# Fourteen elementwise instructions of a two-branch decoder layer moved from VectorE to GpSimd

## Chip, cores and metric

The kernel runs on one core of a Trainium2 chip. The metric is the device time of one execution in microseconds (us). Engines are called as the profile calls them: PE (TensorE, matrix products; PEld is its weight load), DVE (VectorE), ACT (ScalarE), POOL (GpSimd), SP (SyncE, which issues the DMAs). They run side by side, each through its own list of instructions in order, and wait for each other by semaphores.

## What is computed

One layer with two token mixers over the same input, 256 positions by 2048 features, in fp32:

```python
h = rms_norm(x, norm_g)
proj = h @ w_in                                   # (256, 2048) @ (2048, 11264)
q, k, v, z_a, u_b, v_b, z_b, g_a, g_b = split(proj)
att = moba_attention(rms(q), rms(k), v)           # 8 heads, causal, one block here
y_a = (att * silu(z_a)) @ w_proj_a
sgu = gelu(u_b) * (W_s @ rms(gelu(v_b)) + b_s)    # the spatial gating unit
y_b = (sgu * silu(z_b)) @ w_proj_b
merged = sigmoid(g_a) * y_a + sigmoid(g_b) * y_b
return x + merged @ w_out
```

The change touches three elementwise lines of it: the product `gelu(u_b) * mixed`, the product of that with `silu(z_b)`, and the sum of the two gated branches.

## The kernel before

**Products in three parts.** Every weight and every activation is split into a rounded half and the rest (`wh` and `wl`, `xh` and `xl`), and a product is three matrix instructions that accumulate in PSUM. ACT makes the rounded half by a cast (L125, L152, L154), DVE the rest by a subtraction (L126, L155, L157).

**The stream of quads.** The weights come as a stream of pieces of 128 x 2048, 1 MB each, numbered 0, 1, 2, ... by `schedule()`; the number stands in the buffers' names (`wl63`, `tl62`). A quad is four blocks of 128 x 512. Some quads are multiplied directly, 24 instructions (`direct`). The others go through one level of Strassen-Winograd (`seven`, L321), 21 instructions, for which DVE first adds the blocks (`t`: L143, L145, L146) and then makes three remainders: `wlp` (L155) and the two pieces of `tl` (L157), each of 128 x 1024. A direct quad costs DVE one instruction (L126, 128 x 2048), a Strassen quad six.

**Stages.** The columns come in the order q, k, v, za, vb, ub, zb, eight quads each. Then four chunks of 512 output columns follow: eight quads of the two gates (`g`, five of them Strassen) and four pieces of `proj`, the products with w_proj_a and w_proj_b. Last come two rounds of `out`. `early` (L346 to L353) and `final_one` (L361) put together the results of the Strassen quads on DVE.

**The three places of the change.** `spatial` (L491 to L494) multiplies four tiles of 128 x 512 during stage zb. `gate_b` (L496 to L499) multiplies four tiles during the first gate chunk; its result is transposed on PE and split (`turn_z`, L502) in the first `proj`. `merge` (L527 to L536) multiplies both branches with their gates and adds them, two sums in each of four chunks. Their result is transposed by `turn_m` behind the last `proj`.

**What sets the order.** Work is recorded quad by quad in the loop at the end of `hybrid_layer_kernel`. After quad 8 a scheduler decides on each engine's order from its own model of the times, so an edit on one engine can also move instructions on another. The buffers bound how far the engines run ahead: four for `raw` and `t` together, three for `wh` and `th`, three for `wl` and `tl`, two for `whp` and `wlp`.

The four remainders and blocks that the text below names are made here:

```python
nc.scalar.copy(wh[i], r[:, B:])
for sl in (a, b):
    nc.scalar.copy(th[i][:, sl], t[:, sl])
nc.vector.tensor_tensor(wl[i], r[:, B:], f(wh[i]), op=ALU.subtract)
for sl in (a, b):
    nc.vector.tensor_tensor(tl[i][:, sl], t[:, sl], f(th[i][:, sl]), op=ALU.subtract)
```

Of the kernel before, what the change touches and what calls it, by code (L numbers as in the profile page):

```python
# [17 lines left out]
ALU = mybir.AluOpType  # L18
# [49 lines left out]
def hybrid_layer_kernel(  # L68
# [9 lines left out]
    nc = tc.nc  # L78
# [80 lines left out]
    X = {}  # L159
# [331 lines left out]
    def spatial():  # L491
        for m in range(2):
            for c in range(2):
                nc.vector.tensor_tensor(X["ub"][m][c], X["ub"][m][c], X["vb"][m][c], op=ALU.mult)  # L494

    def gate_b():  # L496
        for m in range(2):
            for c in range(2):
                nc.vector.tensor_tensor(X["zb"][m][c], X["zb"][m][c], X["ub"][m][c], op=ALU.mult)  # L499

    def halves(dst_h, dst_l, ps):
        nc.scalar.copy(dst_h, ps)  # L502
# [25 lines left out]
    def merge(c, Y):  # L528

        g = X["g", c]  # L530
        for m in range(2):
            nc.vector.tensor_tensor(g[m][0], Y[m], g[m][0], op=ALU.mult)
        for m in range(2):
            nc.vector.tensor_tensor(g[m][1], Y[2 + m], g[m][1], op=ALU.mult)
            nc.vector.tensor_tensor(g[m][0], g[m][0], g[m][1], op=ALU.add)
        X["m", c] = [g[0][0], g[1][0]]  # L536

    def mm_rows(acc, hl, i, kts, k0, first, last, by_row=False):
# [78 lines left out]
    at(i0 + 0, mix, None)  # L617
    at(i0 + 1, func, "ub", AF.Gelu_apprx_tanh)
    at(i0 + 2, spatial)
    i0 = first["g", 0]  # L620
    at(i0 + 1, func, "zb", AF.Silu)
    at(i0 + 2, gate_b)
    at(first["proj", 0] + 0, turn_z, "zb", "late")
    at(first["proj", 3] + 1, turn_m, 0, "L01")
# [33 lines left out]
    for i, (kind, name, c, kp, n) in enumerate(G):  # L658
# [41 lines left out]
        elif kind == "proj":  # L700
            if n % 2 == 0:
                Y = (Y if n else []) + [bank(E[n + m], f"y{n}_{c}{m}") for m in range(2)]
            z = ("za", "zb")[n // 2]

            def hl(k, m):
                return (X[z + "h"][:, k, m * P:(m + 1) * P], X[z + "l"][:, k, m * P:(m + 1) * P])

            mm_rows(Y[n // 2 * 2:], hl, i, None, 4 * (n % 2), n % 2 == 0, n % 2 == 1)
            if n == 3:
                merge(c, Y)  # L710
# [68 lines left out]
```

## Time and profile before

| what | value |
|---|---|
| runs of the kernel, median | 672.03 us (three: 668.34, 672.03, 673.25) |
| the profiled execution's own time | 668.8 us |
| its span, first to last instruction | 667.0 us |
| mean granted clock of PE, share of full speed | 0.997 |
| PE busy | 655.3 us (98%) |
| DVE busy | 614.2 us (92%) |
| ACT busy | 427.0 us (64%) |
| POOL busy | 32.1 us (5%), 28 instructions |

The span of one execution is what the trace shows; the execution's own time is 1.8 us longer, for what lies around the first and last instruction. A busy PE counts the modelled, overlapping ends of its matmuls, so its waits are better read from the starts of neighbouring instructions.

### The profile page before, as it was taken

What the parts mean: (1) busy time and instruction counts of PE and PEld (TensorE: products, weight loads), DVE (VectorE), ACT (ScalarE), POOL (GpSimd) and SP (SyncE); (2) the same over time, 40 slices, a digit from 0 to 9 for tenths busy, and PEclk for the clock granted to TensorE, in tenths of its full rate; (3) what the DMA queues carried; (4) which work ended last, traced back from release to release, by engine and by line L of the source; (5) the groups of instructions that cost most, each with busy time, mean ns of one, the idle gap of its engine ahead of it and who ended that gap; (6) DMA issues with size and microseconds to landing.
All of it is one profiled execution on the core that took longest, in us unless ns stands there. A gap on an engine that the chain in (4) does not pass through costs nothing.

```text
span 667.0 us, 7852 instructions
## 1 busy us (share of the span) xinstructions
PE 655.3 (98%) x2982; PEld 539.3 (81%) x2982; DVE 614.2 (92%) x605; ACT 427.0 (64%) x562; POOL 32.1 (5%) x28
## 2 busy tenths in 40 slices
PE   8899999999999999999999999999999999999997
PEld 4687788878888888888887888888888888888886
DVE  4499999899999699999999999989979989998996
ACT  7778968856995579674656845554564556746360
POOL 1000501300001004000000000000000000000000
PEclk9899999999999999999999999999999999999999
DMA  8962574455455615744545644845573474747641
GB/s 310 421 225 95 215 255 177 169 220 179 157 200 191 252 65 188 259 178 171 207 146 220 269 167 149 324 151 188 193 294 116 187 273 167 252 143 290 203 185 63
DMA packets 21925, 135.32 MB, mean 203 GB/s; under 512 B 2432, under 2 KB 3072, under 8 KB 6656
## 3 DMA queue, kind: packets, MB, share of 16 engines
q1 hardware_dynamic: 20736, 132.73, 53.8%
q10 hardware_dynamic: 1152, 2.10, 1.0%
q8 instruction: 23, 0.38, 0.2%
q14 instruction: 14, 0.11, 0.0%
HBM read 132.72 MB, written 2.10 MB: 202 GB/s over the span
## 4 chain that ended last, share of the span: by engine, by line
PE 48%; DVE 29%; ACT 8%; issue 8%; DMA 5%; POOL 1%; SPq 0%; DVEq 0%; ACTq 0%
PE acc_g L303 13%; PE y L303 11%; PE acc_out L303 9%; PE seven_g L303 6%; DVE tl L157 6%; DVE wl L126 5%; DMA raw<-in_w 5%; DVE t L143 3%; PE seven_out L303 3%; DVE wlp L155 3%; PE acc_vb L303 3%; ACT wh L125 3%; DVE t L145 2%; DVE t L146 2%; PE seven_vb L303 2%
## 5 line engine op out<-in xcount | busy, mean ns | idle before, releaser
L154 ACT CAST th<-t 128x1024 fp32r<-128x1024 f32 x104 | 109.2, 1053 | 114.5 <-DVE t L143 52.2
L126 DVE TENSOR_TENSOR wl<-raw,wh 128x2048 fp32r<-128x2048 f32 (+2 forms) x75 | 156.0, 2087 | 27.5 <-ACT wh L125 27.2
L125 ACT CAST wh<-raw 128x2048 fp32r<-128x2048 f32 (+2 forms) x75 | 130.8, 1751 | 54.8 <-PE acc_g L303 23.4
L157 DVE TENSOR_TENSOR tl<-t,th 128x1024 fp32r<-128x1024 f32 x104 | 126.1, 1217 | 3.9 <-ACT th L154 3.9
L155 DVE TENSOR_TENSOR wlp<-raw,whp 128x1536 fp32r<-128x1536 f32 x52 | 91.0, 1750 | 4.4 <-ACT whp L152 4.4
L152 ACT CAST whp<-raw 128x1536 fp32r<-128x1536 f32 x52 | 76.8, 1481 | 28.0 <-DMA raw<-in_w 13.0
L143 DVE TENSOR_TENSOR t<-raw 128x1024 f32<-128x1024 f32 x52 | 63.2, 1216 | 0.2
L303 PE MATMUL acc_g<-wh,xh 128*128 128x512 f32 x96 | 37.4, 389 | 0.0
L303 PE MATMUL acc_g<-wh,xl 128*128 128x512 f32 x96 | 37.3, 389 | 0.0
L303 PE MATMUL acc_g<-wl,xh 128*128 128x512 f32 x96 | 37.0, 389 | 0.0
L146 DVE TENSOR_TENSOR t<-t,raw 128x512 f32<-128x512 f32 x52 | 35.8, 689 | 0.3
L145 DVE TENSOR_TENSOR t<-t,raw 128x512 f32<-128x512 f32 x52 | 35.8, 689 | 0.2
L239 POOL TENSOR_TENSOR rs<-ms,mhalf 128x4 f32<-128x4 f32 x12 | 23.7, 1991 | 124.9 <-DVE ms L238 124.9
L303 PE MATMUL acc_q<-wl,xuh 128*128 128x512 f32 x64 | 26.1, 408 | 2.0 <-DVE wl L126 2.0
L303 PE MATMUL acc_q<-wh,xuh 128*128 128x512 f32 x64 | 25.6, 400 | 1.5 <-ACT wh L125 1.5
L303 PE MATMUL acc_q<-wh,xul 128*128 128x512 f32 x64 | 25.9, 404 | 0.8 <-ACT wh L125 0.8
L303 PE MATMUL y<-wh,zbl 128*128 128x512 f32 x64 | 25.1, 392 | 0.0
L303 PE MATMUL y<-wh,zal 128*128 128x512 f32 x64 | 25.0, 390 | 0.0
L303 PE MATMUL y<-wh,zah 128*128 128x512 f32 x64 | 25.0, 390 | 0.0
L303 PE MATMUL y<-wl,zah 128*128 128x512 f32 x64 | 24.9, 389 | 0.0
L303 PE MATMUL y<-wh,zbh 128*128 128x512 f32 x64 | 24.9, 389 | 0.0
L303 PE MATMUL y<-wl,zbh 128*128 128x512 f32 x64 | 24.9, 389 | 0.0
(502 smaller groups left out, 1599.9 us busy)
## 6 DMA issues: line engine op xcount, KB each, us to landing
raw<-in_w SPq DMA_DIRECT2D x117, 1024.0 KB, 4.8
raw<-in_w SPq DMA_DIRECT2D x5, 512.0 KB, 7.7
xnat<-in_x SPq DMA_DIRECT2D x2, 1024.0 KB, 12.7
xres<-in_x ACTq DMA_DIRECT2D x8, 256.0 KB, 4.9
xt<-in_xT SPq DMA_DIRECT2D x3, 512.0 KB, 9.6
out<-out_c SPq DMA_DIRECT2D x5, 256.0 KB, 2.5
raw<-in_w SPq DMA_DIRECT2D x2, 256.0 KB, 4.6
ws<-in_wsT SPq DMA_DIRECT2D x2, 256.0 KB, 2.9
```

What stands on the lines that cost most here:

```text
L125: nc.scalar.copy(h, r)
L126: nc.vector.tensor_tensor(l, r, f(h), op=ALU.subtract)
L143: nc.vector.tensor_tensor(two, r[:, B:3 * B].rearrange("p (a n) -> p a n", a=2), r[:, None, 0:B].to_broadcast([P, 2, B]), op=ALU.add)
L145: nc.vector.tensor_tensor(t[:, 2 * B:3 * B], t[:, 0:B], r[:, 2 * B:3 * B], op=ALU.add)
L146: nc.vector.tensor_tensor(t[:, 3 * B:], t[:, 2 * B:3 * B], r[:, 3 * B:], op=ALU.add)
L152: nc.scalar.copy(wh[i], r[:, B:])
L154: nc.scalar.copy(th[i][:, sl], t[:, sl])
L155: nc.vector.tensor_tensor(wl[i], r[:, B:], f(wh[i]), op=ALU.subtract)
L157: nc.vector.tensor_tensor(tl[i][:, sl], t[:, sl], f(th[i][:, sl]), op=ALU.subtract)
L239: nc.gpsimd.tensor_tensor(dst, ms[:, :n], mhalf[:, :n], op=ALU.pow)
L303: nc.tensor.matmul(acc, a, b, start=(start and n == 0), stop=(stop and n == 2))
```

## The change

Three `nc.vector` calls become `nc.gpsimd` calls: four instructions in `spatial`, four in `gate_b`, and the two sums of `merge` in chunks 0, 1 and 2. In chunk 3 the two sums stay on DVE. Tiles, arithmetic and DMAs are as before.

```diff
     def spatial():
         for m in range(2):
             for c in range(2):
-                nc.vector.tensor_tensor(X["ub"][m][c], X["ub"][m][c], X["vb"][m][c], op=ALU.mult)
+                nc.gpsimd.tensor_tensor(X["ub"][m][c], X["ub"][m][c], X["vb"][m][c], op=ALU.mult)
 
     def gate_b():
         for m in range(2):
             for c in range(2):
-                nc.vector.tensor_tensor(X["zb"][m][c], X["zb"][m][c], X["ub"][m][c], op=ALU.mult)
+                nc.gpsimd.tensor_tensor(X["zb"][m][c], X["zb"][m][c], X["ub"][m][c], op=ALU.mult)
...
         for m in range(2):
             nc.vector.tensor_tensor(g[m][1], Y[2 + m], g[m][1], op=ALU.mult)
-            nc.vector.tensor_tensor(g[m][0], g[m][0], g[m][1], op=ALU.add)
+            (nc.vector if c == 3 else nc.gpsimd).tensor_tensor(g[m][0], g[m][0], g[m][1], op=ALU.add)
```

On DVE, in the middle of the first gate chunk, the four products of `gate_b` stand before among the instructions that prepare quads 60 and 61 (t, wlp, tl and their numbers):

```order
L146 TENSOR_TENSOR t60_2780<-t60_2780,raw60_2743 128x512
L499 TENSOR_TENSOR zb0_c11_2646<-zb0_c11_2646,ub0_c11_2313 128x512
L499 TENSOR_TENSOR zb0_c12_2649<-zb0_c12_2649,ub0_c12_2316 128x512
L157 TENSOR_TENSOR tl60_2787<-t60_2780,th60_2786 128x1024
L499 TENSOR_TENSOR zb0_h_2647<-zb0_h_2647,ub0_h_2314 128x512
L499 TENSOR_TENSOR zb0_c22_2648<-zb0_c22_2648,ub0_c22_2315 128x512
L143 TENSOR_TENSOR t61_2821<-raw61_2778 128x1024
L155 TENSOR_TENSOR wlp61_2826<-raw61_2778,whp61_2825 128x1536
```

Now the same place of DVE's order reads:

```order
L146 TENSOR_TENSOR t60_2780<-t60_2780,raw60_2743 128x512
L155 TENSOR_TENSOR wlp61_2826<-raw61_2778,whp61_2825 128x1536
L157 TENSOR_TENSOR tl60_2787<-t60_2780,th60_2786 128x1024
L143 TENSOR_TENSOR t61_2821<-raw61_2778 128x1024
L145 TENSOR_TENSOR t61_2821<-t61_2821,raw61_2778 128x512
```

The four products are gone from here, and the preparation of quad 61 has closed up. From the start to the second piece of `tl62`, DVE's list holds the same instructions as before less the eight of `spatial` and `gate_b`; that second piece still stands behind `wl63`.

On PE, near the end of the same chunk, quad 62 is the last Strassen quad and quad 63 the direct quad behind it. Before, this is what leads up to the first use of the second piece of `tl62`, the last row here:

```order
L303 MATMUL seven_g0_1_2750<-th62_2867,xl0_424 128x512
L303 MATMUL seven_g0_1_2750<-th62_2867,xh0_423 128x512
L303 MATMUL acc_g0_2_2717<-th62_2867,xl1_349 128x512
L303 MATMUL acc_g0_2_2717<-th62_2867,xh1_348 128x512
L303 MATMUL acc_g0_3_2718<-wh63_2898,xl1_349 128x512
L303 MATMUL acc_g0_3_2718<-wh63_2898,xh1_348 128x512
L303 MATMUL acc_g0_0_2715<-wl63_2899,xh1_348 128x512
L303 MATMUL acc_g0_0_2715<-wh63_2898,xl1_349 128x512
L303 MATMUL acc_g0_0_2715<-wh63_2898,xh1_348 128x512
L303 MATMUL acc_g0_0_2715<-wl63_2899,xh1_348 128x512
L303 MATMUL acc_g0_1_2716<-wl63_2899,xh1_348 128x512
L303 MATMUL seven_g0_1_2750<-tl62_2868,xh0_423 128x512
```

Now PE's order there is the plain one; the second piece of `tl62` is first used in the third row from the end:

```order
L303 MATMUL seven_g0_3_2752<-th62_2867,xl0_424 128x512
L303 MATMUL seven_g0_3_2752<-th62_2867,xh0_423 128x512
L303 MATMUL seven_g0_3_2752<-tl62_2868,xh0_423 128x512
L303 MATMUL seven_g0_2_2751<-th62_2867,xl0_424 128x512
L303 MATMUL seven_g0_2_2751<-th62_2867,xh0_423 128x512
L303 MATMUL seven_g0_2_2751<-tl62_2868,xh0_423 128x512
L303 MATMUL seven_g0_1_2750<-th62_2867,xl0_424 128x512
L303 MATMUL seven_g0_1_2750<-th62_2867,xh0_423 128x512
L303 MATMUL seven_g0_1_2750<-tl62_2868,xh0_423 128x512
L303 MATMUL acc_g0_2_2717<-th62_2867,xl1_349 128x512
```

Thirteen products that stood ahead of the second piece of `tl62` now stand behind it: eleven of quad 63 and two of `acc_g0_2` with `th62`. Counted to the end of the program, 1,290 of the 2,724 products of L303 stand at or behind its first use before, and 1,303 now. SP's order is the same in both. On POOL the fourteen instructions follow each other, behind everything that POOL did before. ACT's order changes by single places.

## Rows read from the trace of the kernel before

**Rows 1.** The page's first part: busy time of each engine, share, instructions.

```profile
PE 655.3 (98%) x2982; PEld 539.3 (81%) x2982; DVE 614.2 (92%) x605; ACT 427.0 (64%) x562; POOL 32.1 (5%) x28
```

**Rows 2.** Busy time of each engine in stretches: from:to, length, engines, clock, DMA.

```profile
core 0: us, PE busy (x) PEld busy (x) DVE busy (x) ACT busy (x) POOL busy (x), PEclk, DMA share, GB/s
...
320.00:340.00 20.00, 20.00 (x90) 16.57 (x89) 19.90 (x22) 13.12 (x13) 0.00 (x0) 1.00 0.45 165
340.00:360.00 20.00, 19.41 (x87) 15.74 (x86) 19.93 (x22) 8.66 (x8) 0.00 (x0) 1.00 0.44 159
360.00:370.00 10.00, 9.68 (x43) 7.70 (x42) 9.66 (x7) 8.15 (x6) 0.00 (x0) 1.00 0.92 359
...
392.00:432.00 40.00, 40.00 (x179) 33.10 (x178) 38.70 (x37) 21.28 (x18) 0.00 (x0) 1.00 0.63 233
...
454.00:494.00 40.00, 40.00 (x178) 33.14 (x177) 37.03 (x36) 21.32 (x18) 0.00 (x0) 1.00 0.63 237
```

**Rows 3.** Timeline of PE, end of the first gate chunk: start, duration, instruction, idle before.

```profile
358.45 0.39 PE L303 MATMUL seven_g<-wlp,xh 128*128 128x512 f32 x1
359.43 0.50 PE L303 MATMUL seven_g<-th,xl 128*128 128x512 f32 x1 [0.59 <-ACT th L154]
...
360.94 0.73 PE L303 MATMUL seven_g<-tl,xh 128*128 128x512 f32 x2 [0.32 <-DVE tl L157]
361.50 0.39 PE L303 MATMUL acc_g<-wh,xl 128*128 128x512 f32 x1
...
364.93 0.39 PE L303 MATMUL seven_g<-tl,xh 128*128 128x512 f32 x1
```

**Rows 4.** Timeline of DVE, stages zb and first gate chunk.

```profile
293.24 0.68 DVE L145 TENSOR_TENSOR t<-t,raw 128x512 f32<-128x512 f32 x1
293.85 1.75 DVE L155 TENSOR_TENSOR wlp<-raw,whp 128x1536 fp32r<-128x1536 f32 x1
...
331.37 0.68 DVE L361 TENSOR_TENSOR zb_c<-acc_zb,zb_c 128x512 f32<-128x512 f32 x1
...
339.31 1.21 DVE L157 TENSOR_TENSOR tl<-t,th 128x1024 fp32r<-128x1024 f32 x1
...
345.59 1.28 DVE L499 TENSOR_TENSOR zb_c<-zb_c,ub_c 128x512 f32<-128x512 f32 x2
346.79 1.22 DVE L157 TENSOR_TENSOR tl<-t,th 128x1024 fp32r<-128x1024 f32 x1
...
363.43 1.22 DVE L157 TENSOR_TENSOR tl<-t,th 128x1024 fp32r<-128x1024 f32 x1
```

**Rows 5.** Groups of POOL: line, form, count | busy us, mean ns | idle before.

```profile
L217 POOL TENSOR_SCALAR_AFFINE_SELECT tri_f<-tri_f 128x512 f32<-128x512 f32 x1 | 0.6, 636 | 0.0
```

**Rows 6.** Instructions on tile ws: count, duration ns min/median/max, first and last start.

```profile
L228 POOL TENSOR_SCALAR_AFFINE_SELECT ws<-ws x2: 1082/1774/2466, 199.5 to 201.9; 128x512 f32<-128x512 f32 x2
```

**Rows 7.** Timeline of DVE beside those two POOL instructions.

```profile
199.07 1.21 DVE L157 TENSOR_TENSOR tl<-t,th 128x1024 fp32r<-128x1024 f32 x1
200.21 1.21 DVE L143 TENSOR_TENSOR t<-raw 128x1024 f32<-128x1024 f32 x1
201.46 1.01 DVE L145 TENSOR_TENSOR t<-t,raw 128x512 f32<-128x512 f32 x1
202.50 1.00 DVE L146 TENSOR_TENSOR t<-t,raw 128x512 f32<-128x512 f32 x1
203.43 1.21 DVE L157 TENSOR_TENSOR tl<-t,th 128x1024 fp32r<-128x1024 f32 x1
```

**Rows 8.** Timeline of ACT: the inputs of the moved products, and the reader of gate_b.

```profile
291.82 2.23 ACT L489 ACTIVATE vb_c<-ps_m,xv 128x128 f32<-128x128 f32 x8
...
330.29 1.23 ACT L403 ACTIVATE zb_c<-zb_c 128x512 f32<-128x512 f32 x2 [2.79 <-DVE zb_c L361]
...
332.08 0.63 ACT L403 ACTIVATE zb_c<-zb_c 128x512 f32<-128x512 f32 x1
...
375.60 1.06 ACT L502 CAST zbh<-ps_zb 128x512 fp32r<-128x512 f32 x2
```

**Rows 9.** Timeline of PE, first use of the second piece of tl58.

```profile
341.00 0.39 PE L303 MATMUL seven_g<-tl,Fhx 128*128 128x512 f32 x1
```

## Prediction

> **What bounds the kernel now.** I read the page's busy shares first. PE is busy 98% of the span and DVE 92% [rows 1]. With two engines that full, the question is where PE waits for DVE, so I went on to the table of stretches. From 320 to 370 us DVE is full (19.90 of 20, 19.93 of 20, 9.66 of 10), and PE loses 0.59 us in 340 to 360 and 0.32 us in 360 to 370. From 392 us on PE is busy in all of each stretch, while DVE has 1.30 us to spare in 392 to 432 and 2.97 us in 454 to 494 [rows 2]. So there is one place behind the middle of the program at which DVE is late: the end of the first gate chunk. Behind it PE sets the time.
>
> PE's timeline shows that place. The products of 128 x 512 follow each other every 0.23 us (fifteen starts from 361.50 up to the one at 364.93 us). Between 358.45 and 361.50 us there are seven starts (two in the row of 360.94), which take 7 x 0.23 = 1.61 us when nothing waits, but 3.05 us pass. PE loses 1.44 us, first to a cast of ACT and then to `tl` of DVE [rows 3]. What DVE does from 280 us to this place carries through to here, for it has no idle time to swallow a delay.
>
> The later piece of the same tile matters for the change. DVE's second `tl` of quad 62 runs from 363.43 to 364.65 us [rows 4], and PE uses it at 364.93 us [rows 3]: 0.28 us to spare.
>
> **What DVE is spared.** The eight products of `spatial` and `gate_b` stand ahead of this place. One costs DVE 0.60 us: a pair of them starts at 345.59 and the next instruction at 346.79 [rows 4]. 8 x 0.60 = 4.8 us less work on DVE. The six sums of `merge` spare it 3.6 us more, but behind 392 us, where PE waits for nothing.
>
> **What GpSimd's work costs DVE.** The trace of before has two POOL instructions of 128 x 512 that read SBUF while DVE is busy, the masks on `ws`. The same form takes 0.636 us when DVE does next to nothing at the start of the program [rows 5]; these two take 2.47 and 1.08 us [rows 6]. DVE pays as well: its two additions of 512 columns beside them last 1.01 and 1.00 us [rows 7] where such an addition lasts 0.68 us [rows 4]. From the start of L143 at 200.21 to the next `tl` at 203.43 us 3.22 us pass [rows 7]. Undisturbed it is 1.14 us for 1024 columns (199.07 to 200.21) [rows 7] and twice 0.61 us for 512 (293.24 to 293.85) [rows 4], 2.36 us together. So two masks cost DVE 0.86 us, 0.43 us each, and the two engines take turns. I call this price c.
>
> A mask reads one tile, the moved products and sums read two. No row shows a two-input POOL instruction of this size. The lower bound is 0.43 us, a mask's price. Twice that, 0.86 us, is the value that I take, since twice as much is read. The upper bound is twice the whole undisturbed mask, 2 x 0.636 = 1.27 us. Below nothing it can't go: GpSimd does not speed DVE up beyond the work taken away. The case that two-input instructions cost DVE nothing at all is a rival below.
>
> How many of the eight pay it? `spatial` has its inputs by about 294 us, `gate_b` between 331 and 333 us [rows 8]; both times DVE's list is full of additions and subtractions with both inputs in SBUF [rows 4]. I count all eight. (The Trainium skill, "SBUF — State Buffer", section "Who interferes with whom", says that a DVE instruction with at most one SBUF input does not contend. The first product of `gate_b` could then run free beside the L361 that read PSUM, until 332 us; by that rule seven pay, and the sum below is 0.9 us lower. No row here shows it.)
>
> **What the changed order costs.** The order of PE loses a cushion. Before, thirteen products of quad 63 and of the th half stood ahead of the second piece of `tl62`; now they stand behind it. PE wants that piece 13 x 0.23 = 3.0 us earlier than before. It had 0.28 us to spare, so with DVE's work unchanged PE would wait 2.7 us more than now. On DVE the piece still stands behind `wl63`, so that its place there brings nothing back.
>
> **The sum.** PE's delay at this place, against before, is 2.7 - 4.8 + 8 c = 8 c - 2.1 us. It can't fall below -1.44 us, the whole wait that there is. With c = 0.86 it is 6.9 - 2.1 = +4.8 us. From there to the end PE works without a wait [rows 2], so the delay goes through to the end.
>
> An earlier place does not add to it. The second piece of `tl58` ends at 340.52 us [rows 4] and is wanted at 341.00 us [rows 9]. By then DVE has lost 8 c but won only the four products of `spatial`, 2.4 us; one product less stands ahead on PE (0.23 us). That is a wait of 6.9 - 2.4 - 0.25 = 4.2 us, there already, and at quad 62 PE then waits for the rest: the later place decides, since its total against an unhindered PE is 4.8 + 1.44 = 6.2 us.
>
> What is hidden: a moved sum costs DVE c - 0.60 = 0.26 us net, the two of a chunk 0.52 us, against 1.30 us and 2.97 us of free time in 40 us [rows 2]. If that cover were gone it would be 3 x 0.52 = 1.6 us. The sums' results are wanted only behind the last `proj`. The result of `gate_b` is read from 375.60 us on [rows 8]; four products that take turns with DVE instructions of 0.68 to 1.75 us [rows 4] need some 4 x (0.86 + 1.75) = 10 us from 333 us, and are done 30 us early. Nothing is queued behind the fourteen on POOL, no DMA is issued or moved, and SP's order is the same.
>
> The profiled execution took 668.8 us, so its like would take 668.8 + 4.8 = 673.6 us. The median of the three runs is 672.0 us, 3.2 us above it; on that base it is 676.8 us. Nothing says which base the next run has, so I forecast between them: 675.5 us, 0.5% to 0.7% longer.
>
> **Rivals.**
>
> 1. *DVE is simply relieved.* GpSimd's products run beside DVE at no cost (c below 0.1). Then 4.8 us are won, the wait of 1.44 us is gone, the changed order on PE costs nothing, and all the rest is PE's: 668.8 - 1.4 = 667.4 us, not slower. For it speaks that DVE is the full engine at just this place and POOL idle [rows 1, 2]. Against it speak the lengthened additions [rows 7]. More than 1.4 us is not to be won, since no later wait is left.
>
> 2. *The turns are dear.* c is 1.1 us or more, since a two-input instruction on GpSimd holds DVE off for as long as it lasts. From c = 1.10 on, 8 c - 2.1 passes 6.7 us, 1%: at c = 1.27 it is +8.1 us, 676.9 us on the profiled base and 680.1 us on the median. The mechanism is the wait of `tl62` alone; its place is the end of the first gate chunk. For it speaks that the mask lasted 2.47 us from start to end [rows 6], against it that DVE itself paid just 0.43 us for one. (The Trainium skill, "GPSIMD Engine Reference", section "Elementwise — side-by-side cycle accounting", gives 4497 ns for an addition of 2048 columns; a quarter, 1.12 us as an estimate, would give 8 x 1.12 - 2.1 = +6.9 us. No row here has that instruction.)
>
> 3. *One read's price.* c stays at 0.43 us: 8 x 0.43 - 2.1 = +1.3 us, 670.1 us. The mask's rows speak for it, the second input against it.
>
> **Chances.** A measurement of this kernel can tell about 1% from no change, some 6.7 us. The forecast (c from 0.6 to 1.1) has 0.5, rival 2 0.27, rival 3 (c from 0.2 to 0.6) 0.14, rival 1 0.09. Slower by over 1%: all of rival 2 and 0.04 of the forecast's upper edge, where the scatter of the runs adds to it, 0.31. Faster by over 1%: only where rival 1 meets a favourable scatter, 0.03. Within 1%: 0.66. The range reaches from rival 3 on the profiled base, 670 us, less 1 us of scatter, to the upper bound on the median's base, 680 us, and 1 us more: 669 to 681 us.
>
> **What would show it.** Right: the POOL products last 1 us and more; DVE's instructions beside them are lengthened as at 201.46 us [rows 7] and the lengthening sums to 5 to 9 us over the eight; PE waits for `tl` at 341 and again near 362 us, over 5 us in all in place of 1.44; from the first `proj` to the end the time is what it was. Wrong: DVE's instructions keep their lengths beside POOL and PE's wait at 360 us is gone (rival 1); or PE waits in the later chunks, which would say that the cover of the sums was too thin; or the wait at quad 62 is gone although DVE is late, which would say that my count of the order is wrong.

## The result, and the profile after

| what | before | after |
|---|---|---|
| median of 16 runs each | 672.12 us (668.34 to 673.25) | 676.39 us (674.63 to 681.88) |
| after divided by before, with 95% interval | | 1.0103 [1.0079, 1.0126] |
| the profiled execution's span | 667.0 us | 673.7 us |

The kernel became slower by 1.0%. The runs of each kernel fall into two groups (medians 668.5 and 672.8 us before, 675.6 and 680.4 us after), and like held against like is 1.011 in both, while the two medians of the table come from different groups and their quotient, 1.006, says too little. The spans say the same as the ratio, 673.7 / 667.0 = 1.010.

The first part of the page, to be held against [rows 1]:

```profile
PE 656.1 (97%) x2982; PEld 539.2 (80%) x2982; DVE 619.8 (92%) x591; ACT 427.1 (63%) x562; POOL 64.6 (10%) x42
```

DVE has fourteen instructions fewer (591 against 605) and is busy 5.6 us more. That alone says that the work taken off it came back as longer instructions.

**Where the time went.** PE works through the same 2,724 products of L303, in an order that is nearly the same, so three products can serve as milestones: the first of the gates (`acc_g`), the first of `proj` (`y`), and the first that uses `zbl`. PE's timeline of the kernel before:

```profile
326.71 0.39 PE L303 MATMUL acc_g<-wh,xl 128*128 128x512 f32 x1
...
368.33 0.39 PE L303 MATMUL y<-wh,zal 128*128 128x512 f32 x1
...
381.00 0.39 PE L303 MATMUL y<-wh,zbl 128*128 128x512 f32 x1
```

And of the kernel after, with the waits between them (in brackets: idle time, and what ended it):

```profile
325.97 0.39 PE L303 MATMUL acc_g<-wh,xl 128*128 128x512 f32 x1
...
329.26 0.50 PE L303 MATMUL acc_g<-wh,xl 128*128 128x512 f32 x1 [0.41 <-DVE zb_h L352]
...
341.47 0.50 PE L303 MATMUL seven_g<-tl,Fhx 128*128 128x512 f32 x1 [1.54 <-DVE tl L157]
...
343.16 0.50 PE L303 MATMUL seven_g<-th,Flx 128*128 128x512 f32 x1 [0.49 <-ACT th L154]
...
345.41 0.50 PE L303 MATMUL seven_g<-tl,Fhx 128*128 128x512 f32 x1 [1.52 <-DVE tl L157]
...
366.70 0.50 PE L303 MATMUL seven_g<-tl,xh 128*128 128x512 f32 x1 [1.27 <-DVE tl L157]
...
373.18 0.39 PE L303 MATMUL y<-wh,zal 128*128 128x512 f32 x1
...
387.52 0.50 PE L303 MATMUL y<-wh,zbl 128*128 128x512 f32 x1 [1.27 <-DVE zbl L503]
```

Three differences make the whole:

- Up to the first product of the gates: 325.97 - 326.71 = -0.74 us. Stage zb, in which GpSimd makes the products of `spatial`, takes PE 44.39 us in this kernel and 44.38 in the one before; the 0.74 us come from the stages ahead of it, which no edit touches. That start varies from one execution to the next (324.8 to 331.4 us over the kernels of this study).
- The first gate chunk, to the first `y`: 47.21 us in place of 41.62, +5.59 us. Before, PE waited for a cast of ACT and for `tl` of DVE near its end [rows 3]; now it waits at five places, and four of the five releasers are DVE's. (Products of 0.39 us start 0.23 us apart, and the one behind a wait lasts 0.50 us, so each wait costs some 0.27 us more than its bracket. Counted by the starts of the products, PE loses 7.03 us in this chunk, and 1.44 us before.)
- From the first `y` to the end: 300.55 us in place of 298.71 (673.73 - 373.18 and 667.04 - 368.33), +1.84 us. The wait in it is the one of 1.27 us for `zbl`, in the first `proj`.

Together -0.74 + 5.59 + 1.84 = +6.7 us, the difference of the spans.

The table of stretches shows the same, beside [rows 2] (from:to, length, then busy us of PE, PEld, DVE, ACT, POOL, the clock and the DMAs):

```profile
320.00:340.00 20.00, 19.45 (x84) 15.06 (x82) 19.96 (x19) 12.87 (x13) 7.66 (x4) 1.00 0.36 133
340.00:360.00 20.00, 16.52 (x70) 13.07 (x71) 19.93 (x19) 9.73 (x9) 0.33 (x1) 1.00 0.43 157
360.00:370.00 10.00, 8.73 (x38) 6.89 (x38) 9.90 (x8) 6.41 (x5) 0.00 (x0) 1.00 0.88 328
...
380.00:390.00 10.00, 8.73 (x42) 6.69 (x41) 9.43 (x8) 7.23 (x8) 0.00 (x0) 1.00 0.23 94
...
392.00:432.00 40.00, 40.00 (x178) 33.14 (x177) 37.66 (x33) 20.91 (x17) 2.99 (x2) 1.00 0.56 210
```

DVE is as full as before from 320 to 370 us but gets through fewer instructions (19, 19 and 8 where it was 22, 22 and 7), and PE is busy in only 16.52 of the 20 us from 340 on. From 392 us on PE waits for nothing, as before. The granted clock is 1.00 in all these stretches.

**How GpSimd and DVE met.** POOL's timeline of the kernel after:

```profile
289.33 8.39 POOL L494 TENSOR_TENSOR ub_c<-ub_c,vb_c 128x512 f32<-128x512 f32 x1 [28.62 <-ACT vb_c L489]
297.68 2.28 POOL L494 TENSOR_TENSOR ub_h<-ub_h,vb_h 128x512 f32<-128x512 f32 x1
299.91 5.58 POOL L494 TENSOR_TENSOR ub_c<-ub_c,vb_c 128x512 f32<-128x512 f32 x2
332.34 3.54 POOL L499 TENSOR_TENSOR zb_c<-zb_c,ub_c 128x512 f32<-128x512 f32 x2 [26.84 <-ACT zb_c L403]
...
399.51 1.29 POOL L535 TENSOR_TENSOR g_c<-g_c,g_c 128x512 f32<-128x512 f32 x1 [59.17 <-DVE g_c L534]
```

And DVE's, beside them:

```profile
295.33 3.46 DVE L157 TENSOR_TENSOR tl<-t,th 128x1024 fp32r<-128x1024 f32 x2
298.83 2.21 DVE L143 TENSOR_TENSOR t<-raw 128x1024 f32<-128x1024 f32 x1
300.97 3.38 DVE L126 TENSOR_TENSOR wl<-raw,wh 128x2048 fp32r<-128x2048 f32 x1
304.27 1.78 DVE L145 TENSOR_TENSOR t<-t,raw 128x512 f32<-128x512 f32 x1
...
332.65 0.68 DVE L361 TENSOR_TENSOR zb_c<-acc_zb,zb_c 128x512 f32<-128x512 f32 x1
333.25 1.47 DVE L143 TENSOR_TENSOR t<-raw 128x1024 f32<-128x1024 f32 x1
334.64 2.85 DVE L155 TENSOR_TENSOR wlp<-raw,whp 128x1536 fp32r<-128x1536 f32 x1
...
337.42 1.78 DVE L145 TENSOR_TENSOR t<-t,raw 128x512 f32<-128x512 f32 x1
339.12 2.30 DVE L157 TENSOR_TENSOR tl<-t,th 128x1024 fp32r<-128x1024 f32 x1
```

A product that started while DVE ran an instruction that reads PSUM was not stretched: 1.29 us at 399.51 (beside L534) and 1.30 us for the first of `gate_b` at 332.34. The other seven of the eight took 1.73 to 8.39 us, and DVE's instructions beside them are stretched too, one for each. Against their undisturbed lengths (L143 1.21 and `tl` 1.21 [rows 7], L145 0.68 and L155 1.75 [rows 4], L126 2.28) the eight are longer by 1.1, 1.00, 1.10 and 1.10 us beside `spatial`, and by 0.26, 1.10, 1.10 and 1.09 us beside `gate_b`: 7.85 us in all, 0.98 us for one product. The 0.26 us belong to the first product of `gate_b`, part of whose time lay beside the L361 of 332.65, which reads PSUM and one SBUF tile and kept its 0.68 us. (The Trainium skill, "SBUF — State Buffer", section "Who interferes with whom", says that a DVE instruction with at most one SBUF input doesn't contend with GpSimd. The trace agrees: the L361 lasts 0.68 us beside a GpSimd product, as it does without one [rows 4].)

### The profile page after: what moved, and what is told of

Its sections match the earlier page's. It is cut to its first block, busy times and chain, and to the rows that moved or that the text cites. A ratio compares the mean times of both kernels' runs of the same rounds, so it can differ in the third digit from the quotient of the medians.

```text
span 673.7 us, 7895 instructions
## 1 busy us (share of the span) xinstructions
PE 656.1 (97%) x2982; PEld 539.2 (80%) x2982; DVE 619.8 (92%) x591; ACT 427.1 (63%) x562; POOL 64.6 (10%) x42
## 4 chain that ended last, share of the span: by engine, by line
PE 56%; DVE 22%; issue 7%; ACT 7%; DMA 5%; POOL 0%; SPq 0%; DVEq 0%; ACTq 0%
PE acc_g L303 14%; PE acc_out L303 9%; PE y L303 9%; PE seven_g L303 7%; DMA raw<-in_w 5%; PE acc_ub L303 4%; DVE wl L126 4%; DVE tl L157 4%; PE seven_out L303 3%; PE acc_vb L303 3%; ACT wh L125 3%; DVE wlp L155 2%; DVE t L143 2%; PE acc_zb L303 2%; PE seven_ub L303 2%
## 5 line engine op out<-in xcount | busy, mean ns | idle before, releaser
L126 DVE TENSOR_TENSOR wl<-raw,wh 128x2048 fp32r<-128x2048 f32 (+2 forms) x75 | 157.2, 2103 | 29.1 <-ACT wh L125 28.4
L157 DVE TENSOR_TENSOR tl<-t,th 128x1024 fp32r<-128x1024 f32 x104 | 131.4, 1271 | 3.3 <-ACT th L154 3.2
L155 DVE TENSOR_TENSOR wlp<-raw,whp 128x1536 fp32r<-128x1536 f32 x52 | 92.2, 1773 | 4.5 <-ACT whp L152 4.5
L143 DVE TENSOR_TENSOR t<-raw 128x1024 f32<-128x1024 f32 x52 | 64.6, 1243 | 0.4
L145 DVE TENSOR_TENSOR t<-t,raw 128x512 f32<-128x512 f32 x52 | 39.6, 762 | 0.3
L303 PE MATMUL acc_g<-wh,xl 128*128 128x512 f32 x96 | 37.6, 391 | 0.5 <-DVE zb_h L352 0.4
L303 PE MATMUL acc_g<-wh,xh 128*128 128x512 f32 x96 | 37.4, 389 | 0.0
L303 PE MATMUL acc_g<-wl,xh 128*128 128x512 f32 x96 | 37.4, 389 | 0.0
L146 DVE TENSOR_TENSOR t<-t,raw 128x512 f32<-128x512 f32 x52 | 36.6, 705 | 0.3
L239 POOL TENSOR_TENSOR rs<-ms,mhalf 128x4 f32<-128x4 f32 x12 | 22.1, 1857 | 124.9 <-DVE ms L238 124.9
L303 PE MATMUL acc_q<-wl,xuh 128*128 128x512 f32 x64 | 25.6, 400 | 2.7 <-DVE wl L126 2.7
L303 PE MATMUL acc_q<-wh,xuh 128*128 128x512 f32 x64 | 25.8, 403 | 1.4 <-ACT wh L125 1.4
L303 PE MATMUL y<-wh,zbl 128*128 128x512 f32 x64 | 25.2, 393 | 1.3 <-DVE zbl L503 1.3
L303 PE MATMUL acc_q<-wh,xul 128*128 128x512 f32 x64 | 25.8, 402 | 0.2 <-ACT wh L125 0.2
L303 PE MATMUL y<-wh,zal 128*128 128x512 f32 x64 | 25.1, 392 | 0.0
L303 PE MATMUL y<-wl,zah 128*128 128x512 f32 x64 | 25.0, 391 | 0.0
L303 PE MATMUL y<-wh,zbh 128*128 128x512 f32 x64 | 24.9, 389 | 0.0
L303 PE MATMUL y<-wl,zbh 128*128 128x512 f32 x64 | 24.9, 389 | 0.0
L303 PE MATMUL y<-wh,zah 128*128 128x512 f32 x64 | 24.9, 389 | 0.0
```

The lines of the kernel that those rows point to most:

```text
L126: nc.vector.tensor_tensor(l, r, f(h), op=ALU.subtract)
L143: nc.vector.tensor_tensor(two, r[:, B:3 * B].rearrange("p (a n) -> p a n", a=2), r[:, None, 0:B].to_broadcast([P, 2, B]), op=ALU.add)
L145: nc.vector.tensor_tensor(t[:, 2 * B:3 * B], t[:, 0:B], r[:, 2 * B:3 * B], op=ALU.add)
L146: nc.vector.tensor_tensor(t[:, 3 * B:], t[:, 2 * B:3 * B], r[:, 3 * B:], op=ALU.add)
L239: nc.gpsimd.tensor_tensor(dst, ms[:, :n], mhalf[:, :n], op=ALU.pow)
L303: nc.tensor.matmul(acc, a, b, start=(start and n == 0), stop=(stop and n == 2))
```

## The experiments

The theory: DVE pays about 1 us for each moved product, and with the changed order of PE that makes the delay in the first gate chunk; a second delay, of the first `proj`, comes from the order alone. Rivals: the new order of the engines makes most of the delay, whatever GpSimd does; or the sums of `merge` take part in it.

Times of PE are given as two stretches between the milestones, as differences from the kernel before (41.62 us for the first gate chunk, 298.71 us for the rest), of one profiled execution of each. Stage zb took 44.38 or 44.39 us in all of them.

| kernel | span | first gate chunk | rest | ratio with 95% interval |
|---|---|---|---|---|
| after | 673.7 | +5.59 | +1.84 | 1.0103 [1.0079, 1.0126] |
| e5_copy | 672.2 | +0.30 | +1.89 | 1.0049 [1.0016, 1.0082] |
| e6_memset | 666.8 | -1.50 | +1.85 | 1.0007 [0.9977, 1.0036] |
| e7_turn | 670.8 | +6.01 | -0.29 | 1.0080 [1.0050, 1.0111] |
| e3_sums | 667.0 | +0.01 | +0.05 | 0.9991 [0.9962, 1.0021] |
| e1_spatial | 674.2 | +2.28 | +0.24 | 1.0053 [1.0018, 1.0088] |
| e2_gate | 671.0 | +3.54 | +0.86 | 1.0049 [1.0013, 1.0084] |
| e9_late | 666.0 | -1.38 | +1.25 | 0.9991 [0.9959, 1.0024] |

The two columns say more than the spans. The start of the first gate chunk lies between 324.8 and 331.4 us in these executions, from what happened before any edit takes effect, and a span carries that scatter.

**Copies in place of the products (e5_copy).** Against the kernel after:

```diff
-                nc.gpsimd.tensor_tensor(X["ub"][m][c], X["ub"][m][c], X["vb"][m][c], op=ALU.mult)
+                nc.gpsimd.tensor_copy(X["ub"][m][c], X["vb"][m][c])
...
-                nc.gpsimd.tensor_tensor(X["zb"][m][c], X["zb"][m][c], X["ub"][m][c], op=ALU.mult)
+                nc.gpsimd.tensor_copy(X["zb"][m][c], X["ub"][m][c])
```

Expected:

> The eight GpSimd products of the changed kernel are replaced by eight GpSimd copies of the same tiles (ub from vb, zb from ub), so the multiplication is left out and one input is read in place of two. All other engines have exactly the changed kernel's order. Theory A (what DVE pays is the time for which a GpSimd instruction reads SBUF): about 0.43 us a copy, as for the masks, so DVE loses 3.4 us in place of 7.8 us; PE's waits between 320 and 370 us sum to some 2.8 us in place of 6.9 us; with the new wait for zbl in the first proj (1.8 us) the span is 3 us above before, ratio 1.004 to 1.006. Rival B (the changed order on PE and DVE is the cause, not what GpSimd does): waits and ratio as in the changed kernel, 1.010.

PE, DVE, ACT and SP have the same order as in the kernel after. DVE beside the copies:

```profile
299.13 2.77 DVE L157 TENSOR_TENSOR tl<-t,th 128x1024 fp32r<-128x1024 f32 x2
...
301.93 1.52 DVE L143 TENSOR_TENSOR t<-raw 128x1024 f32<-128x1024 f32 x1
303.37 2.69 DVE L126 TENSOR_TENSOR wl<-raw,wh 128x2048 fp32r<-128x2048 f32 x1
305.98 1.09 DVE L145 TENSOR_TENSOR t<-t,raw 128x512 f32<-128x512 f32 x1
...
333.69 0.68 DVE L361 TENSOR_TENSOR zb_c<-acc_zb,zb_c 128x512 f32<-128x512 f32 x1
```

A copy costs DVE 0.41 us where it meets an instruction with two SBUF inputs for its whole length (0.42, 0.31, 0.41 and 0.41 us here). The first two copies of `gate_b` started beside the L361; they cost 0.15 us together and took 0.615 us each:

```profile
L499 POOL COPY zb_c<-ub_c x3: 615/616/2136, 333.4 to 336.1; 128x512 f32<-128x512 f32 x3
```

All eight copies cost 2.5 us, less than the 3.4 us expected, and PE loses 1.7 us in the chunk in place of the 2.8 us expected, since these two hardly paid. The prediction's formula, with 2.5 us in place of 8 c, gives 2.7 - 4.8 + 2.5 = +0.4 us; measured +0.30 us in the first gate chunk. So a whole turn costs DVE 1.1 us beside a product of two tiles and 0.41 us beside a copy of one; the two differ in the second input and in the operation, and no run parts these. The rest of the program is as late as in the kernel after, +1.89 us.

**Fills in place of the products (e6_memset).** The same two lines of the kernel after, now:

```diff
+                nc.gpsimd.memset(X["ub"][m][c], 0.5)
...
+                nc.gpsimd.memset(X["zb"][m][c], 0.5)
```

Expected:

> The eight GpSimd products of the changed kernel are replaced by eight GpSimd memsets of the same output tiles, so the products are left out and GpSimd reads nothing. All other engines have exactly the changed kernel's order. Theory A: DVE's instructions keep their lengths beside the memsets, PE's waits between 320 and 370 us sum to less than 0.5 us (1.45 us before, 6.9 us in the changed kernel); the wait for zbl in the first proj stays at 1.4 to 1.9 us, since it comes of the order; the span is that of before plus 0 to 0.5 us, ratio 0.999 to 1.002. Rival B (order alone): waits of 5 us and more, ratio 1.010.

POOL's instructions on `zb_c` (count, ns shortest/median/longest), in which nothing is read from SBUF:

```profile
L499 POOL MEMSET zb_c<- x3: 526/526/527, 328.5 to 330.3; 128x512 f32 x3
```

DVE in the same microseconds:

```profile
329.42 1.22 DVE L143 TENSOR_TENSOR t<-raw 128x1024 f32<-128x1024 f32 x1
330.55 1.75 DVE L155 TENSOR_TENSOR wlp<-raw,whp 128x1536 fp32r<-128x1536 f32 x1
332.21 0.69 DVE L145 TENSOR_TENSOR t<-t,raw 128x512 f32<-128x512 f32 x1
```

DVE keeps its undisturbed lengths, and the first gate chunk is 1.50 us shorter than before. The formula gives -2.1 us, but no more than the wait there was, 1.44 us, can be won. So the order of the kernel after is not slow by itself in this chunk: the rival that put the delay down to the order falls. But the rest stays +1.85 us, though DVE kept PE waiting nowhere in the first gate chunk. PE, after the first gate chunk:

```profile
380.58 0.50 PE L303 MATMUL y<-wh,zbl 128*128 128x512 f32 x1 [1.28 <-DVE zbl L503]
```

Products, copies or fills, this wait is 1.27 or 1.28 us and the rest +1.84 to +1.89 us. It comes of the order, not of the price that DVE pays.

**Another order around `zbl` (e7_turn).** Against the kernel after, in the loop that records the work:

```diff
-            fn(*a)
+            if fn is turn_z and a[0] == "zb":
+                with tc.high_priority():
+                    fn(*a)
+            else:
+                fn(*a)
```

Expected:

> The changed kernel with turn_z of zb recorded at a high priority, so that its transposes, casts and subtractions stand earlier in the first proj; up to there all orders are the changed kernel's. Theory A: the wait for zbl (1.4 us, 1.8 us with what goes with it) comes of the order in the first proj and is gone; the waits between 320 and 370 us stay at 6.9 us; ratio 1.007 to 1.009. Rival C (PE waits for zbl because DVE comes late out of the first gate chunk): the wait stays, ratio 1.010.

The table of stretches, with the kernel before in the last row:

```profile
360.00:370.00 10.00, 8.75 (x39) 6.88 (x38) 9.89 (x9) 5.36 (x4) 0.00 (x0) 1.00 0.96 361
370.00:392.00 22.00, 22.00 (x106) 18.25 (x105) 20.74 (x21) 14.89 (x15) 0.00 (x0) 1.00 0.51 187
...
370.00:392.00 22.00, 22.00 (x107) 18.40 (x106) 21.90 (x24) 14.55 (x17) 0.00 (x0) 1.00 0.54 199
```

PE is busy through all of 370 to 392 us, the wait for `zbl` is gone, and the rest is -0.29 us against before. The first gate chunk is as late as ever (+6.01 us; four transposes of PE now stand ahead of its last milestone, and they account for the 0.42 us above the kernel after). Both stretches together are +5.72 us in place of +7.43 us, so 1.71 us are won. So the two delays are separate, and each has its own cause. The order is not that of before: it has the transposes, casts and L503 earlier than either kernel. The two ratios, 1.0080 and 1.0103, are too close for their intervals to tell the kernels apart; the milestones do it.

What the order of the kernel after did there is to be seen on DVE. The kernel before ran the second pair of L503 (the remainders of z_b's transposes) directly behind a `wl`:

```profile
377.42 2.28 DVE L126 TENSOR_TENSOR wl<-raw,wh 128x2048 fp32r<-128x2048 f32 x1
379.62 1.28 DVE L503 TENSOR_TENSOR zbl<-ps_zb,zbh 128x512 fp32r<-128x512 f32 x2
```

The kernel after has both `wl` first, and L143 and L155 of quad 69 between the two pairs:

```profile
380.57 2.29 DVE L126 TENSOR_TENSOR wl<-raw,wh 128x2048 fp32r<-128x2048 f32 x1 [2.34 <-ACT wh L125]
382.79 1.28 DVE L503 TENSOR_TENSOR zbl<-ps_zb,zbh 128x512 fp32r<-128x512 f32 x2
383.98 1.22 DVE L143 TENSOR_TENSOR t<-raw 128x1024 f32<-128x1024 f32 x1
385.12 1.75 DVE L155 TENSOR_TENSOR wlp<-raw,whp 128x1536 fp32r<-128x1536 f32 x1
386.79 1.28 DVE L503 TENSOR_TENSOR zbl<-ps_zb,zbh 128x512 fp32r<-128x512 f32 x2
```

Before, the third L503 ended near 380.3 us (379.62 and one of 0.68 us) and PE wanted its first product of `zbl` at 381.00 us: 0.7 us to spare. After, the third ends near 387.5 us, and that product starts at 387.52 us. That it is the third, and not the two that wrote the operand, follows from the code: the accumulators of the z_b half take the PSUM banks that the transposes use (L702, L723), and the third L503 is the last reader of the bank wanted first. No run tests this last step.

**The sums of `merge` alone (e3_sums).** Against the kernel before:

```diff
-            nc.vector.tensor_tensor(g[m][0], g[m][0], g[m][1], op=ALU.add)
+            (nc.vector if c == 3 else nc.gpsimd).tensor_tensor(g[m][0], g[m][0], g[m][1], op=ALU.add)
```

Expected:

> Only the six sums of merge go to GpSimd, the eight products stay on DVE; PE's order is that of before. Theory A: each pair of sums lengthens two or three DVE instructions by some 2 us in all in place of 1.2 us of work, in stretches where PE has no wait and DVE has 1.3 to 3 us of free time in 40 us; no new PE wait, ratio 0.999 to 1.001. Rival D (the sums' turns are part of the loss): PE waits of 0.5 to 2 us in the gate chunks 1 to 3, ratio 1.002 to 1.008.

The table of stretches:

```profile
392.00:432.00 40.00, 40.00 (x178) 33.16 (x177) 39.52 (x35) 21.20 (x18) 2.99 (x2) 1.00 0.62 235
```

The stretch is one of [rows 2]: DVE is busy 39.52 of 40 us (38.70 before), and PE loses nothing. The ratio, 0.9991, is no change that can be measured. The sums have no part in the result.

**`spatial` alone and `gate_b` alone (e1_spatial, e2_gate).** Each is the kernel before with one of the two edits:

```diff
-                nc.vector.tensor_tensor(X["ub"][m][c], X["ub"][m][c], X["vb"][m][c], op=ALU.mult)
+                nc.gpsimd.tensor_tensor(X["ub"][m][c], X["ub"][m][c], X["vb"][m][c], op=ALU.mult)
```

```diff
-                nc.vector.tensor_tensor(X["zb"][m][c], X["zb"][m][c], X["ub"][m][c], op=ALU.mult)
+                nc.gpsimd.tensor_tensor(X["zb"][m][c], X["zb"][m][c], X["ub"][m][c], op=ALU.mult)
```

Expected of the first:

> Only the four products of spatial go to GpSimd. Theory A (delay at quad 62 = what GpSimd's turns cost DVE, less the work taken from DVE, plus 0.23 us for each product of PE that no longer stands ahead of the piece awaited): turns 4.3 us as in the changed kernel, less 2.4 us, plus 0.23 us, since 1,291 products stand behind the second piece of tl62 against 1,290 before: +2.1 us, so PE's waits between 320 and 370 us sum to 3.4 to 3.7 us; no wait for zbl, since the first proj has the order of before; ratio about 1.003. Rival E (PE's lost cushion is not a term, DVE's net loss alone counts): 3.3 us, hardly apart here; rival F (any product on GpSimd costs the full 5.6 us, since the order breaks): 7 us.

Expected of the second:

> Only the four products of gate_b go to GpSimd. Theory A: turns 3.5 us as in the changed kernel (the first product runs beside DVE instructions that read PSUM), less 2.4 us, plus 5 x 0.23 us less the 0.28 us to spare, since 1,295 products stand behind the second piece of tl62: +2.0 us, PE's waits between 320 and 370 us 3.2 to 3.6 us; a wait for zbl of 0.5 to 1.5 us, since DVE's order there has both wl ahead of the first zbl; ratio 1.003 to 1.005. Rival E (no term for PE's order): +1.1 us, waits 2.5 us.

`spatial` alone makes the first gate chunk 2.28 us longer, and the rest 0.24 us. Its POOL products are those of the kernel after (8.42 us for the first, held off in the same way). The large span, 674.2 us, is not the edit's: PE was busy only 7.07 of the 10 us from 130 to 140 us, in stage v, long before any moved product (the table of stretches):

```profile
130.00:140.00 10.00, 7.07 (x28) 4.59 (x27) 9.52 (x9) 6.08 (x5) 0.00 (x0) 1.00 0.62 222
140.00:150.00 10.00, 10.00 (x39) 8.08 (x38) 9.93 (x12) 4.94 (x4) 0.00 (x0) 0.83 0.66 264
```

`gate_b` alone makes the first gate chunk 3.54 us longer and the rest 0.86 us, so the second delay comes in the main with the move of `gate_b`: PE waits 0.42 us for `zbl` there, less than the 0.5 to 1.5 us expected, and not at all with `spatial` alone. The two make 1.10 us of the 1.84; the remainder comes only with both edits together. About 1.6 us of the 3.54 are a fall of the clock (last section). Without it, the parts alone would give 2.28 and, as an estimate, 1.9 us, 4.2 together against 5.59 for both. The order fits that: counted to the end, 1,290 products stood at or behind the first use of the second piece of `tl62` before; with both edits it is 1,303, with `spatial` alone 1,291, with `gate_b` alone 1,295. The formula with each one's own numbers (lengthened turns, less 2.4 us, plus 0.23 us for each product of cushion, less the 0.28 us to spare) gives 4.30 - 2.4 + 0.23 - 0.28 = 1.9 us and 3.55 - 2.4 + 1.15 - 0.28 = 2.0 us, where the turns are taken from the kernel after. Only both edits together cost the whole cushion of 13. These two sums agree in size only, for in neither run did PE wait for the second piece of `tl62`: it was there 0.28 and 0.30 us early. With `spatial` alone the last wait of the chunk is one of 0.98 us for `tl61`, with `gate_b` alone one of 1.28 us for `tl58`. What bears out the cushion better are the kernel after and e5_copy, where PE's last wait, of 1.27 us both times, is for that piece: without the 2.7 us the formula would give 7.85 - 4.8 = +3.05 and 2.5 - 4.8 = -2.3 us, and +5.59 and +0.30 us were measured. No run puts the cushion back by itself.

**`gate_b` later on DVE (e9_late).** If the one wait of the kernel before is all there is to win, moving DVE's work behind it should win it. Against the kernel before:

```diff
-    at(i0 + 2, gate_b)
+    at(i0 + 7, gate_b)
```

Expected:

> Nothing on GpSimd; the kernel before with gate_b recorded five quads later, so that on DVE one of its four products stands ahead of quad 62 in place of four. Theory A: 1.8 us less work ahead of quad 62 on DVE, 3 to 2 products of PE fewer ahead: the wait at quad 62 falls from 1.45 us to 0 to 0.3 us. The work is not gone, though: it stands ahead of zbl, and there the kernel before has next to nothing to spare, so a wait for zbl of about 1 us takes its place; ratio 0.998 to 1.001. Rival: zbl has time to spare and 1.4 us are won, ratio 0.998.

The table of stretches:

```profile
360.00:370.00 10.00, 10.00 (x46) 8.25 (x45) 8.85 (x10) 7.55 (x5) 0.00 (x0) 1.00 1.01 393
370.00:390.00 20.00, 19.35 (x93) 15.47 (x92) 20.00 (x22) 12.17 (x13) 0.00 (x0) 1.00 0.49 167
```

The wait at the end of the first gate chunk is gone (-1.38 us), and DVE is late for `zbl` in the first `proj` in its place (+1.25 us): DVE full, 20.00 of 20 us, PE 19.35. Won and given back; no version of this study beats the kernel before by what can be measured.

## Why the prediction was right and wrong

- *PE waits for DVE at one place, the end of the first gate chunk, and what DVE loses ahead of it comes out there.* Right. It came out as the prediction had it, first at `tl58` (wanted near 341 us, then waits of 1.54 and 1.52 us), and the rest at `tl62` (1.27 us).
- *All eight products pay, and PE's order loses a cushion: the delay is 8 c - 2.1 us.* Right in form. With the price measured as 7.85 us, 2.5 us and nothing it gives +5.75, +0.4 and -2.1 us (cut to -1.44); the chunk was +5.59, +0.30 and -1.50 us. One of the eight hardly paid, the one beside L361.
- *c = 0.86 us.* This term was mis-sized: 0.98 us on the mean, 1.0 to 1.1 us for each full turn. It made the delay 5.59 us where the sum had 4.8. The two masks [rows 6, 7] were a poor measure: they read one tile and are another operation. The copy, with one input too, costs 0.41 us, about the mask's 0.43; the two-input product costs not twice that but 1.1.
- *The two engines take turns.* Right, once it started. Not foreseen was that the first product of `spatial` found no turn for 8.39 us, while DVE went from one instruction straight into the next. Its result was wanted late enough that this cost nothing.
- *"From there to the end PE works without a wait [rows 2], so the delay goes through to the end."* This step failed. The term for what comes behind the first gate chunk was put at nothing, and it measured +1.84 us. The rows used had no idle PE behind 392 us, and that stayed true; but between, in the first `proj`, DVE was busy 21.90 of the 22 us from 370 on and PE's margin to the third L503 was 0.7 us, and the scheduler's new order used it up and made PE wait 1.27 us more. I had followed the new order to the first use of `tl62`, and not on to the next place where PE reads something that DVE makes in the moved neighbourhood. The run e7_turn shows the price of this omission: of the 1.84 us, 1.71 are won with the work on `zbl` recorded earlier.
- *The sums are hidden; the result of `gate_b` is in time.* Right: e3_sums lost 0.06 us, and the last product of `gate_b` ended near 340 us, over 30 us before it is read.
- *Within 1% as the likeliest.* The profiled sum was 4.8 us. It lacked 0.8 us of the price and 1.84 us of the order, and 0.74 us came back from the scatter of the early stages: 4.8 + 0.8 + 1.8 - 0.7 = 6.7 us, just over 1% of 667. That the forecast of 675.5 us lies close to the measured 676.39 us is luck: it stood between two bases, 6.7 us above one and 3.5 us above the other. As a difference the sum was too small by more than a quarter, and the 0.5% to 0.7% that was forecast came out as 1.0%.
- *Rival 2, the turns are dear (c from 1.10 us on), slower by over 1%.* Its condition was met by single full turns, its mean was not reached; without the delay in the first `proj` the change would be +5.6 us, 0.8%. The run without it, e7_turn, has 1.0080.

## What to carry to other kernels

An elementwise instruction moved from a full DVE to an idle GpSimd is not work saved: here one product was worth 0.60 us to DVE and cost it 0.98 us, because DVE's own instructions beside it read two SBUF tiles. Move work to a place where DVE's neighbours read PSUM or where PE has slack (the sums here), and price it from an instruction of the same kind, with as many inputs. And where a scheduler decides the order, follow its new order to every later place at which the waiting engine has little margin, not only to the one that waits now.

## What the runs showed of the hardware that was not expected

- A GpSimd product was kept out as long as DVE ran without a gap: 8.39 us in the kernel after and 8.42 us in e1_spatial, over several DVE instructions, and it got in where a gap came, between two `tl`: the second waited for its cast on ACT and started 1.21 us behind the first, where such starts stand 1.14 us apart [rows 7]. From then on the engines alternated, one product between two DVE instructions. Whoever plans with such a product should reckon with a start that can be late by a whole burst of DVE.
- The price for DVE by what GpSimd reads, beside DVE instructions with two SBUF inputs: 1.0 to 1.1 us for a 128 x 512 product of two tiles (1.29 us beside DVE instructions that read PSUM), 0.31 to 0.42 us for a copy of one (0.615 us in the same way), nothing for a fill (0.526 us).
- In e2_gate PE's clock fell. The granted clock was 0.52, which is about the lower of its two levels (1.2 of 2.4 GHz), for the 3.3 us behind a stretch in which PE waited 0.62, 0.49 and 1.28 us:

```profile
337.00:344.50 7.50, 5.11 (x20) 3.31 (x19) 7.50 (x6) 1.31 (x2) 1.56 (x1) 0.98 0.39 140
344.50:347.80 3.30, 3.30 (x9) 2.53 (x8) 3.30 (x4) 2.42 (x2) 0.00 (x0) 0.52 0.85 318
```

Eight products stand 0.43 us apart there, in place of 0.23 us: 8 x 0.20 = 1.6 us. The kernel after has waits of 1.54, 0.49 and 1.52 us at the same place without such a fall. What makes the difference is open.
